# Running sums' rows by DMA through memory, and state space groups outside the job queue

## The chip, the core and the metric

The kernel runs on one core of a Trainium2 chip. The metric is device time in microseconds (us), as the median of several runs. The engines are named PE (TensorE, matmuls), DVE (VectorE), ACT (ScalarE), POOL (GpSimd) and SP (SyncE, which issues most of the DMAs).

## What is computed

Two models are run one after the other on 256 tokens of width 1024, two layers each. The change is in the first. One layer of it projects the normed input and runs three branches, whose gated outputs are projected, summed and added to the residual:

```python
# state space branch, 16 heads in 4 groups, chunks of 128
a_cum = cumsum(dt * a)                          # over the chunk
seg = a_cum[..., :, None] - a_cum[..., None, :]
decay = where(causal, exp(where(causal, seg, 0)), 0)
cb = einsum('bclgn,bcsgn->bgcls', C, B)         # per group
y_diag = einsum(cb * decay, x_dt)               # per head
...
cum = cumsum(log_sigmoid(f_logit + f_bias))
sc = q @ k * scale + cum[query] - cum[key]
probs = softmax(where(causal, sc, -inf)); out = probs @ v
# the third branch is sliding window attention with sinks, without running sums
```

Both running sums are needed twice per element of a 128 x 384 tile (the causal blocks of a 256 x 256 matrix): one as a column, one number per partition, and one as a row that is the same in all partitions. The change is about the rows.

## The kernel before

**Products.** Activations lie with features on partitions. Every product with a weight is taken in split precision: SP loads a unit of weights (8 blocks of 128 by 256 columns, 1 MB) into `wr` (line 123, three buffers), ACT copies it rounded into `wh`, four chunks of 128x512 (line 98), and DVE, for one chunk POOL, subtracts to get `wl` (line 101). `mm3` then makes three matmuls per block, so a unit is 48 matmuls of 128x256. The loads are issued two units ahead of their use.

**Order.** PE keeps the order in which the program is written. What is not a weight product is woven in by ticks: after each 12 matmuls `tick` advances time by 0.5, steps the tasks whose `yield` has run out, and advances the job queue. So one unit of `yield` is 24 matmuls. The other engines' orders come from a scheduler; each engine runs its own order strictly.

**Jobs.** An attention job (`attn4`) for two heads has stages A (scores into PSUM, masked reduction on DVE, exponentials on ACT, normalisation on DVE), B (transposes on PE), 2.5 after A, and C (product with v), 1 after B. Next to B the following job's A is called.

**Running sums.** `steps_task` makes step sizes and log decays (`u`, `y`, 64 x 256), waits with `yield 7`, transposes them on PE, and makes the sums with triangular matmuls. The result `rows` (128 x 384) is kept as two rounded parts, high and low, on separate partitions. A row is spread over all partitions by a matmul with a column of `selr`, a 0/1 matrix: lines 725 to 729 for attention, where the scores are then accumulated on top of it, and line 844 in `group_task`, where `ps` then goes through DVE (line 848, minus the column, at most 0).

**State space groups.** For each of four groups the loop at the end of `b1_layer` computes `xs`, then B and C (`bcm`), then the gate `z`, each a weight unit. `conv` turns the first two into 128x512 tiles: per half one ACT step and three DVE steps, then a tanh on ACT and a last DVE product. Then `group_task` is spawned. It transposes `xs` (line 95), multiplies C with B (`ps<-f`), and hands two jobs to the job queue, which make the decays of two heads each, and in their C stage the product with `xs`, `po<-f,f`. After these come the norm of the group (`rs_r`) and its spreading over partitions (`pt<-cst,rs_r`), which the products with `ya` need.

In the names of the rows, `f` is any tile of the pool `f2` (13 buffers of 128x512 here), `pd`, `ps`, `pt` and `po` are PSUM tiles, `h` is the normed input, `yb` the sliding window branch's output.

Of the kernel before, what the change touches and what calls it, by code (L numbers as in the profile page):

```python
# [24 lines left out]
def _pack(table, items):  # L25
    o = 0
    for name, n in items:
        table[name] = (o, n)
        o += n
    return o  # L30
# [8 lines left out]
NCST = _pack(CST, [("ident", 128), ("tri", 128), ("ntri", 128), ("sel", 32), ("hl", 1),  # L39
                   ("sgn", 1), ("ca", 1), ("cf", 1), ("msel", 24)])  # L40
# [6 lines left out]
class Kern:  # L47
    def __init__(self, ctx, tc, A, out, dbg=None):
        self.tc, self.nc, self.A, self.out = tc, tc.nc, A, out
        self.dbg = dbg or {}  # L50
        nc = tc.nc
        self.V, self.S, self.P, self.T = nc.vector, nc.scalar, nc.gpsimd, nc.tensor
        p = lambda name, bufs, **kw: ctx.enter_context(tc.tile_pool(name=name, bufs=bufs, **kw))
        self.cst_p = p("cst", 1)
        self.w_p = p("w", 3)
        self.wl_p = p("wlo", 3)
        self.x_p = p("x", 1)
        self.m_p = p("wm", 2)
        self.r_p = p("r", 3)
        self.sm_p = p("sm", 2)  # L60
        self.ps_d = p("psd", 3, space=PSUM)
        self.ps_s = p("pss", 2, space=PSUM)
        self.ps_t = p("pst", 2, space=PSUM)
        self.ps_o = p("pso", 1, space=PSUM)
        self.t = self.rows = 0
        self.on_pool = (1024,)
        self.tasks = []
        self.jobs = []
        self.waiting = []
        self.cur = self.nxt = None  # L70
# [123 lines left out]
    def advance(self):  # L194

        c = self.cur
        if c is None:
            if self.jobs:
                self.start()
        elif c.stage == 0:  # L200
            if self.t - c.t >= 2.5:
                if c.B is None:
                    c.C()
                    self.cur = None
                    self.start()
                else:
                    c.B()
                    c.stage, c.t = 1, self.t
                    if self.jobs:
                        self.nxt = self.jobs.pop(0)  # L210
                        self.nxt.A()
                        self.nxt.t = self.t
        elif self.t - c.t >= 1:
            c.C()
            self.cur, self.nxt = self.nxt, None
            if self.cur is None:
                self.start()

    def start(self):
        if self.jobs:  # L220
            self.cur = self.jobs.pop(0)
            self.cur.A()
            self.cur.t = self.t

    def qk(self, pss, cuts, q, k, first):

        for a, b, c, d in cuts:
            for i, ps in enumerate(pss):
                p = slice(64 * i, 64 * i + 64)
                self.mm(ps[:, a:b], q[p, 128 * (a > 0):128 * (a > 0) + 128], k[p, c:d], first, first or b == 384)  # L230
# [68 lines left out]
    def consts(self):  # L299
        nc, A = self.nc, self.A  # L300
        c = self.cst_p.tile([128, NCST], F32, name="cst")
        nc.sync.dma_start(c, A["cst"])
        g = lambda n: c[:, CST[n][0]:CST[n][0] + CST[n][1]]
        self.ident, self.tri, self.ntri = g("ident"), g("tri"), g("ntri")
        self.hl, self.sgn, self.ca, self.cf = g("hl"), g("sgn"), g("ca"), g("cf")
        self.msel = g("msel")
        self.sel = self.cst_p.tile([128, 32], F32R, name="selr")
        self.V.tensor_copy(self.sel, g("sel"))
# [168 lines left out]
class Job:  # L477


    def __init__(self, A, B, C):  # L480
        self.A, self.B, self.C, self.stage, self.t = A, B, C, 0, 0
# [20 lines left out]
def b1_layer(K, l, x, yr, sums, cw, wdt=None, first_sums=None):  # L502
# [41 lines left out]
    rows = K.sm1_p.tile([128, 384], F32R, name="rows")  # L544
# [3 lines left out]
    def steps_task():  # L548
# [5 lines left out]
        if first_sums is not None:  # L554
            yield 4
# [23 lines left out]
        yield 7  # L579
# [17 lines left out]
        rh = K.f2((128, 384), F32R)  # L597
        K.act(rh, ps)
        K.stt(rows, rh.bitcast(F32), K.hl, ps, ALU.mult, ALU.add)
# [19 lines left out]
    def pv2(o, pair, v, pts):  # L619
        for i in range(2):  # L620
            K.mm(o[64 * i:64 * i + 64, pair, :], v(i, 0), pts[i][:, 0:256], True, False)
        for i in range(2):
            K.mm(o[64 * i:64 * i + 64, pair, 128:256], v(i, 1), pts[i][:, 256:384], False, True)

    def attn4(score, v, masks, mn_fix, done, wait=0, until=()):
# [5 lines left out]
        def job(pair):  # L631
            def A():
                mn = K.small([128, 2, 2], "mn")
# [5 lines left out]
                for i, ps in enumerate(pss):  # L639
                    pr = K.f2((128, 384))  # L640
                    for a, s in enumerate((slice(0, 128), slice(128, 384))):
                        K.masked(pr[:, s], ps[:, s], masks[a], mn[:, i, a:a + 1],
                                 3e38 if mn_fix is None else ns[:, i:i + 1])
                    prs.append(pr)
# [17 lines left out]
            def B():  # L662
                pts = []
                for i, pr in enumerate(sh["p"]):
# [8 lines left out]
                    pts.append(pT)  # L673
# [10 lines left out]
            return Job(A, B, C)  # L684
# [13 lines left out]
    for i in range(4):  # L698
# [26 lines left out]
        def score(pair, pss, q=q, kk=kk, i=i):  # L725
            for e, ps in enumerate(pss):
                o = 16 + 4 * i + 2 * pair + e
                K.mm(ps, K.sel[:, o:o + 1].to_broadcast([128, 128]), rows, True, False)
            K.qk(pss, ((0, 128, 0, 128), (128, 384, 0, 256)), q[:, pair, :], kk[:, pair, :], False)

        jc += attn4(score, lambda j, t, v=v: v[:, t, 64 * j:64 * j + 64], (K.msk("u"), K.msk("zero", 2)), None, gated(yc, zs, 2 * i),
                    until=(steps,))

# [48 lines left out]
    for i in range(4):  # L782
# [7 lines left out]
        def score(pair, pss, q=q, i=i):  # L790
            K.qk(pss, ((0, 128, 0, 128), (128, 384, 0, 256)), q[:, pair, :], kk[:, i // 2, :], True)
# [27 lines left out]
    def group_task(g, xs, bcm, zs):  # L819
# [16 lines left out]
        sh = {}  # L836

        def job(pair):
            def A():
                sh["m", pair] = ms = []  # L840
                for i in range(2):
                    hd = 4 * g + 2 * pair + i
                    ps = K.psx((128, 384))
                    K.mm(ps, K.sel[:, hd:hd + 1].to_broadcast([128, 128]), rows, True, True)
                    m = K.f2((128, 384))

                    for t, s in enumerate((slice(0, 256), slice(256, 384))):
                        V.tensor_scalar(m[:, s], ps[:, s], ncum[:, t, hd:hd + 1], 0.0, op0=ALU.add, op1=ALU.min)  # L848
                    K.act(m, m, AF.Exp)
                    K.tt(m, m, cb, ALU.mult)  # L850
                    ms.append(m)

            def C():
                if pair == 0:
                    return
                o = K.po((128, 2, 256))
                for pr in range(2):
                    pv2(o, pr, lambda i, t: xd[:, t, 64 * (2 * pr + i):64 * (2 * pr + i) + 64], sh["m", pr])
                t1 = K.f2((128, 2, 256))
                for c in range(2):  # L860
                    K.stt(t1[:, c, :], xs[:, c, :], vec("dsk", 8 * l + 2 * g + c), o[:, c, :], ALU.mult, ALU.add)
                y = K.k_p.tile([128, 2, 256], F32, name="yg%d" % g, tag="k%d" % g)
                K.stt(y, t1, 0.5, zs, ALU.mult, ALU.mult)
                sh["y"] = y
                K.act(t1, y, AF.Square)
                K.tt(t1[:, 0, :], t1[:, 0, :], t1[:, 1, :], ALU.add, K.P)
                sh["sq"] = t1

            return Job(A, None, C)

        yield 1
        K.enqueue([job(0), job(1)])
        while "sq" not in sh:
            yield 1
        yield 2
        ps = K.pt((128, 2))
        for t in range(2):
            K.mm(ps[:, t:t + 1], sh["sq"][:, 0, t * 128:t * 128 + 128], K.ones[:, 0:1], True, True)
# [4 lines left out]
        K.tt(t1, sh["y"], K.bc(R, 2), ALU.mult)  # L883
# [7 lines left out]
    for g in range(4):  # L891
        xs = conv(K.dense(K.unit(), H, (0, 1)), (2 * g, 2 * g + 1))
        bcm = conv(K.dense(K.unit(), H, (0, 1)), (8 + g, 12 + g))
        zs = gate_z(K.dense(K.unit(), H, (0, 1)))
        gts.append(K.spawn(group_task(g, xs, bcm, zs)))
# [821 lines left out]
def layout(inputs):  # L1717
# [21 lines left out]
    sel = np.zeros((128, 32), f32)  # L1739
    for h in range(16):  # L1740
        sel[[h, 32 + h], h] = 1
        sel[[64 + h, 96 + h], 16 + h] = 1
    p = np.arange(128)
    hl = np.where((p // 32) % 2 == 1, -1, 0).astype(f32)
# [3 lines left out]
    cst = {"ident": I, "tri": (i <= j).astype(f32), "ntri": -(i > j).astype(f32), "sel": sel,  # L1748
           "hl": hl[:, None], "sgn": sgn[:, None], "ca": ca[:, None], "cf": cf[:, None], "msel": (p[:, None] % 32 == np.arange(24)[None, :]).astype(f32)}
# [167 lines left out]
```

## Time and profile before

| what | value |
|---|---|
| median of three runs | 2091.35 us (2088.39 to 2092.54) |
| the profiled execution, and its span | 2090.28 us, 2088.5 us |
| granted clock of PE, mean | 0.995 |
| busy: PE, DVE, ACT, POOL | 2044.8, 1457.0, 991.1, 482.1 us |
| DMA | 326.12 MB, 156 GB/s |
| layer 0, layer 1 state space groups | about 285 to 425 us, 770 to 905 us |

Busy time tells how much an engine did, over stages that have different limits. To know what a change of one stage is worth, the windows of that stage are read, and in it who waits for whom. A timeline row gives the start, the time taken by a group of like instructions (from the first start to the last end), and in brackets how long the engine had been idle before it and what ended that. Matmuls overlap each other by their filling, so distances between starts tell what one costs.

### The profile page before, as it was taken

The page shows a single profiled execution, that of the slowest core. Times are in us where ns is not written, and L with a number is a line of the kernel's source. Part 1 is how long each engine was busy: PE and PEld are TensorE (multiplying, and loading weights), DVE is VectorE, ACT ScalarE, POOL GpSimd, SP SyncE. Part 2 cuts the span into 40 slices and gives each one's busy share as a digit, 9 for nine tenths or more (in the row PEclk, how much of TensorE's full clock was granted, in tenths as well). Part 3 has the DMA queues.
Part 4 walks back from the last instruction along what each step waited for, and adds up shares of the span by engine and source line. Part 5 has one row for each costly group of instructions (what it writes and reads, how often), then busy time and mean ns, then how long its engine had stood idle before and what let it go on. Part 6 is the DMA issues. An engine that isn't in the chain of part 4 may idle for free.

```text
span 2088.5 us, 37547 instructions
## 1 busy us (share of the span) xinstructions
PE 2044.8 (98%) x14832; PEld 1850.8 (89%) x14832; DVE 1457.0 (70%) x2837; ACT 991.1 (47%) x2117; POOL 482.1 (23%) x361
## 2 busy tenths in 40 slices
PE   7999999999999999999999999999999989999998
PEld 7988999998988999999877888888888889999998
DVE  7667788866766778978466454864565566779974
ACT  6455555544454555555244333542333354556553
POOL 3222222323113223233100212111111131232222
PEclk9999999999999999999999999999999999999999
DMA  7645656565646656544111232222322233454552
GB/s 276 247 162 195 229 190 235 182 242 187 232 172 207 218 184 226 192 177 179 59 56 56 86 121 101 89 93 101 101 101 79 83 132 112 144 190 162 184 181 81
DMA packets 52831, 326.12 MB, mean 156 GB/s; under 512 B 6832, under 2 KB 8624, under 8 KB 16304
## 3 DMA queue, kind: packets, MB, share of 16 engines
q1 hardware_dynamic: 48528, 319.26, 43.2%
q10 hardware_dynamic: 4128, 4.46, 0.8%
q8 instruction: 117, 1.92, 0.4%
q14 instruction: 58, 0.48, 0.1%
HBM read 318.72 MB, written 1.05 MB: 153 GB/s over the span
## 4 chain that ended last, share of the span: by engine, by line
PE 89%; DVE 6%; DMA 2%; issue 1%; ACT 1%; ACTq 0%; POOL 0%; SPq 0%; DVEq 0%; POOLq 0%
PE pd L92 77%; PE ps L92 4%; PE po L92 3%; DVE wl L101 2%; PE pt L92 2%; PE pt L95 2%; DMA f<-f 1%; DVE f L101 1%; DVE f L104 1%; ACT wh L98 1%; ACT f L98 0%; DMA wr<-in_w_dram 0%; DVE rq_t L104 0%; DVE f L969 0%; ACTq L1037 0%
## 5 line engine op out<-in xcount | busy, mean ns | idle before, releaser
L101 DVE TENSOR_TENSOR wl<-wr,wh 128x512 fp32r<-128x512 f32 x751 | 676.3, 920 | 253.0 <-ACT wh L98 251.5
L98 ACT ACTIVATE wh<-wr 128x512 fp32r<-128x512 f32 x992 | 561.3, 621 | 531.3 <-PE pd L92 299.0
L101 POOL TENSOR_TENSOR wl<-wr,wh 128x512 fp32r<-128x512 f32 x241 | 351.0, 1456 | 1311.5 <-ACT wh L98 1125.9
L92 PE MATMUL pd<-h,wh 128*128 128x256 f32 x2688 | 497.3, 286 | 1.8 <-ACT wh L98 1.8
L92 PEld LDWEIGHTS pd<-h,wh 128*128 128x128 f32 x2688 | 419.2, 192 | 22.2 <-issue 17.3
L92 PE MATMUL pd<-h,wl 128*128 128x256 f32 x1344 | 380.6, 283 | 2.5 <-DVE wl L101 2.5
L92 PE MATMUL pd<-hh,wh 128*128 128x512 f32 (+1 forms) x992 | 345.9, 349 | 0.1
L92 PE MATMUL pd<-hh,wl 128*128 128x512 f32 (+1 forms) x992 | 339.7, 342 | 3.0 <-DVE wl L101 3.0
L92 PE MATMUL pd<-hl,wh 128*128 128x512 f32 (+1 forms) x992 | 340.0, 343 | 1.9 <-DVE hl L101 1.9
L92 PEld LDWEIGHTS pd<-h,wl 128*128 128x128 f32 x1344 | 258.1, 192 | 2.7 <-DVE wl L101 2.7
L92 PEld LDWEIGHTS pd<-hh,wh 128*128 128x128 f32 x992 | 188.9, 190 | 28.7 <-issue 7.5
L92 PEld LDWEIGHTS pd<-hh,wl 128*128 128x128 f32 x992 | 189.0, 191 | 24.8 <-DVE wl L101 3.4
L92 PEld LDWEIGHTS pd<-hl,wh 128*128 128x128 f32 x992 | 189.1, 191 | 22.8 <-DVE hl L101 2.3
L92 PE MATMUL pd<-act,wh 128*128 128x256 f32 (+1 forms) x688 | 161.9, 329 | 2.7 <-DVE f L104 2.7
L104 DVE SCALAR_TENSOR_TENSOR f<-pd,cw,f 128x255 f32<-128x255 f32 (+3 forms) x272 | 151.2, 556 | 15.7 <-ACT f L98 13.0
L92 PEld LDWEIGHTS pd<-act,wh 128*128 128x128 f32 x688 | 117.4, 192 | 14.0 <-ACT wh L98 2.9
L92 PE MATMUL pd<-mg,wh 128*128 128x256 f32 (+1 forms) x576 | 113.7, 296 | 2.8 <-DVE mg L104 2.1
L92 PE MATMUL pd<-hf,wh 128*128 128x256 f32 x640 | 115.4, 283 | 0.0
L92 PE MATMUL pd<-act,wl 128*128 128x256 f32 (+1 forms) x344 | 112.8, 328 | 0.0
L98 ACT ACTIVATE f<-f,mn 128x128 f32<-128x128 f32 (+2 forms) x160 | 79.7, 500 | 59.6 <-DVE mn L234 59.5
L92 PEld LDWEIGHTS pd<-hf,wh 128*128 128x128 f32 x640 | 99.8, 192 | 0.1
L98 ACT ACTIVATE f<-f 128x512 f32<-128x512 f32 (+4 forms) x92 | 52.3, 568 | 99.5 <-DVE f L848 50.5
(259 smaller groups left out, 3238.7 us busy)
## 6 DMA issues: line engine op xcount, KB each, us to landing
wr<-in_w_dram SPq DMA_DIRECT2D x233, 1024.0 KB, 4.8
wm<-in_wm_dram SPq DMA_DIRECT2D x48, 1024.0 KB, 7.9
wr<-in_wd_dram SPq DMA_DIRECT2D x8, 768.0 KB, 4.2
wr<-in_wa_dram SPq DMA_DIRECT2D x8, 512.0 KB, 3.5
c<-in_c_dram SPq DMA_DIRECT2D x2, 1920.0 KB, 9.3
f<-f ACTq DMA_DIRECT2D x32, 64.0 KB, 2.1
wr<-in_wp_dram SPq DMA_DIRECT2D x8, 256.0 KB, 2.6
wr<-in_wf_dram SPq DMA_DIRECT2D x8, 256.0 KB, 2.6
```

What stands on the lines that cost most here:

```text
L92: self.T.matmul(out, l, r, start=start, stop=stop)
L95: self.T.transpose(out, in_, self.ident[0:k, 0:k])
L98: self.S.activation(out, in_, f, **kw)
L101: (eng or self.V).tensor_tensor(out, a, b, op=op)
L104: self.V.scalar_tensor_tensor(out, a, s, b, op0=op0, op1=op1)
```

## The change

`rows` becomes a plain float32 tile. SP writes it to a tile `far` in device memory, and each row that is wanted is read back by SP with a source that repeats over 128 partitions. `selr` and the high and low parts go.

Attention: a new stage P of a job issues the two copies of its heads (128x384, 196 KB each) and lets POOL add the causal mask to the diagonal blocks. P is called 0.5 after the A of the job ahead, and A not before 2 after P. The scores start their own PSUM group, and the masked reduction takes the copy as its second operand.

State space: the groups no longer use the job queue. `group_task` is spawned before the gate's unit, with a wait of 0.5, and first issues three copies: two of 2 heads by 256 and one of 4 heads by 128. One unit later come the transposes and the product of C and B, then three steps of 0.5 that turn the three copies into decays, each one exponential and one product over 512 columns, and after 1.5 more the product with `xs`. `z` is handed over through a dictionary. In `steps_task` the waits go from 4 to 3 (first layer alone) and from 7 to 5.5.

```diff
     def advance(self):
...
         elif c.stage == 0:
+            if self.t - c.t >= 0.5:
+                self.prepared()
             if self.t - c.t >= 2.5:
-                if c.B is None:
...
-                else:
-                    c.B()
-                    c.stage, c.t = 1, self.t
-                    if self.jobs:
-                        self.nxt = self.jobs.pop(0)
...
+                c.B()
+                c.stage, c.t = 1, self.t
+                if self.prepared():
+                    self.nxt = self.jobs.pop(0)
...
+    def prepared(self):
+        if not self.jobs:
+            return False
+        j = self.jobs[0]
+        if j.P is None:
+            return True
+        if j.since is None:
+            j.P()
+            j.since = self.t
+        return self.t - j.since >= 2
...
-    rows = K.sm1_p.tile([128, 384], F32R, name="rows")
+    rows = K.sm1_p.tile([128, 384], F32, name="rows")
+    far = K.dram_p.tile([128, 384], F32, name="far%d" % l)
+    def spread_row(n):
+        t = K.f2((128, 384))
+        nc.sync.dma_start(t, far[n:n + 1, :].to_broadcast([128, 384]))
+        return t
...
         if first_sums is not None:
-            yield 4
+            yield 3
...
-        yield 7
+        yield 5.5
...
-        rh = K.f2((128, 384), F32R)
-        K.act(rh, ps)
-        K.stt(rows, rh.bitcast(F32), K.hl, ps, ALU.mult, ALU.add)
+        K.act(rows, ps)
+        nc.sync.dma_start(far, rows)
...
+            def P():
+                sh["b"] = [spread_row(row0 + 2 * pair + i) for i in range(2)]
+                for t in sh["b"]:
+                    diag = t.rearrange("p (a b) -> p a b", a=3)[:, 0:3:2, :]
+                    K.tt(diag, diag, K.bc(K.msk("u"), 2), ALU.add, K.P)
...
         def score(pair, pss, q=q, kk=kk, i=i):
-            for e, ps in enumerate(pss):
-                o = 16 + 4 * i + 2 * pair + e
-                K.mm(ps, K.sel[:, o:o + 1].to_broadcast([128, 128]), rows, True, False)
-            K.qk(pss, ((0, 128, 0, 128), (128, 384, 0, 256)), q[:, pair, :], kk[:, pair, :], False)
+            K.qk(pss, ((0, 128, 0, 128), (128, 384, 0, 256)), q[:, pair, :], kk[:, pair, :])
...
-    def group_task(g, xs, bcm, zs):
+    def group_task(g, xs, bcm, zd):
+        dec = []
+        for hs, cs in ((2, slice(0, 256)), (2, slice(0, 256)), (4, slice(256, 384))):
+            h0 = 4 * g + (2 if len(dec) == 1 else 0)
+            t = K.f2((128, hs, cs.stop - cs.start))
+            nc.sync.dma_start(t, far[h0:h0 + hs, cs].unsqueeze(0).to_broadcast([128, hs, cs.stop - cs.start]))
+            dec.append(t)
         yield 1
...
         yield 1
-        K.enqueue([job(0), job(1)])
-        while "sq" not in sh:
-            yield 1
+        for n in (0, 2, 1):
+            m = dec[n]
+            for i in range(m.shape[1]):
+                hd = 4 * g + i + (2 if n == 1 else 0)
+                V.tensor_scalar(m[:, i, :], m[:, i, :], ncum[:, n // 2, hd:hd + 1], 0.0, op0=ALU.add, op1=ALU.min)
+            K.act(m, m, AF.Exp)
+            K.tt(m, m, K.bc(cb[:, 256:384] if n == 2 else cb[:, 0:256], m.shape[1]), ALU.mult)
+            yield 0.5
+        yield 1.5
+        while "z" not in zd:
+            yield 0.5
+        o = K.po((128, 2, 256))
...
         bcm = conv(K.dense(K.unit(), H, (0, 1)), (8 + g, 12 + g))
-        zs = gate_z(K.dense(K.unit(), H, (0, 1)))
-        gts.append(K.spawn(group_task(g, xs, bcm, zs)))
+        zd = {}
+        gts.append(K.spawn(group_task(g, xs, bcm, zd), 0.5))
+        zd["z"] = gate_z(K.dense(K.unit(), H, (0, 1)))
         gate_proj(1, yb, g, jb, False)
```

PE, before, second group of layer 0, at the end of the gate's unit (products with `h`) and the start of the branch projection (products with `yb`). `f_3803` is `xs`, `f_3902` is `bcm`:

```order
L92 MATMUL pd<-h,wh 128x256 x2
L92 MATMUL pd<-h,wl 128x256
L95 MATMUL pt<-cst,f_3803 128x128 x4
L92 MATMUL ps<-f_3902 128x256
L92 MATMUL ps<-f_3902 128x128
L92 MATMUL pd<-yb,wh 128x256 x2
```

PE, after, the same group, 36 matmuls into the unit of z, the first behind the unit of B and C. `f_3847` is `xs`, `f_3930` is `bcm`:

```order
L92 MATMUL pd<-h,wh 128x256 x2
L92 MATMUL pd<-h,wl 128x256
L95 MATMUL pt<-cst,f_3847 128x128 x4
L92 MATMUL ps<-f_3930 128x256
L92 MATMUL ps<-f_3930 128x128
L92 MATMUL pd<-h,wh 128x256 x2
```

The transposes and the product of C and B moved from the end of the gate's unit to 60 matmuls earlier, into z's.

DVE, before, the same group: the convolution of B and C, `f_3893`, to its last product `f_3902`; `po` and `yg` belong to the group ahead:

```order
L101 TENSOR_TENSOR wl<-wr,wh 128x512 x2
L104 SCALAR_TENSOR_TENSOR f_3886<-f_3385,vec_108,po 128x256 x2
L104 SCALAR_TENSOR_TENSOR f_3893<-pd,cw_195,f_3893 128x255
L104 SCALAR_TENSOR_TENSOR yg_3889<-f_3886,f_3561 128x512
L104 SCALAR_TENSOR_TENSOR f_3893<-pd,cw_195,f_3893 128x254
L101 TENSOR_TENSOR wl<-wr,wh 128x512
L104 SCALAR_TENSOR_TENSOR f_3893<-pd,cw_195,f_3893 128x253
L104 SCALAR_TENSOR_TENSOR f_3893<-pd,cw_195,f_3893 128x255
L104 SCALAR_TENSOR_TENSOR f_3893<-pd,cw_195,f_3893 128x254
L104 SCALAR_TENSOR_TENSOR f_3893<-pd,cw_195,f_3893 128x253
L101 TENSOR_TENSOR wl<-wr,wh 128x512 x2
L104 SCALAR_TENSOR_TENSOR f_3902<-f_3902,f_3893 128x512
```

DVE, after, the same convolution, `f_3921`, to its last product `f_3930`:

```order
L101 TENSOR_TENSOR wl<-wr,wh 128x512
L104 SCALAR_TENSOR_TENSOR f_3921<-pd,cw_195,f_3921 128x255
L101 TENSOR_TENSOR wl<-wr,wh 128x512
L104 SCALAR_TENSOR_TENSOR f_3921<-pd,cw_195,f_3921 128x254
L101 TENSOR_TENSOR wl<-wr,wh 128x512
L104 SCALAR_TENSOR_TENSOR f_3921<-pd,cw_195,f_3921 128x253
L104 SCALAR_TENSOR_TENSOR f_3921<-pd,cw_195,f_3921 128x255
L104 SCALAR_TENSOR_TENSOR f_3921<-pd,cw_195,f_3921 128x254
L104 SCALAR_TENSOR_TENSOR f_3921<-pd,cw_195,f_3921 128x253
L101 TENSOR_TENSOR f_3961<-yg_3739,pt 128x512
L104 SCALAR_TENSOR_TENSOR f_3930<-f_3930,f_3921 128x512
```

Skip term and gate of the group ahead have left the place; three chunks of weights' low parts stand between the first steps, and the norm of the group ahead, `f_3961`, before the last product.

PE, before, a second pair of heads of the forgetting attention, layer 0: transposes of the pair ahead, the rows by `selr`, the scores:

```order
L95 MATMUL pt<-cst,f_1245 128x128 x3
L95 MATMUL pt<-cst,f_1248 128x128 x3
L92 MATMUL ps<-rows,selr 128x384 x2
L92 MATMUL ps<-f_552,f_551 128x128 x2
L92 MATMUL ps<-f_552,f_551 128x256 x2
L92 MATMUL pd<-h,wh 128x256 x2
```

PE, after, the same pair; `f_1157` and `f_1159` are the spread rows, which the pair ahead's scores were reduced into:

```order
L95 MATMUL pt<-cst,f_1157 128x128 x3
L95 MATMUL pt<-cst,f_1159 128x128 x3
L92 MATMUL ps<-f_553,f_552 128x128 x2
L92 MATMUL ps<-f_553,f_552 128x256 x2
L92 MATMUL pd<-h,wh 128x256 x2
```

The two matmuls with `selr` are gone, and the order around them stays.

## Rows read from the trace of the kernel before

**Rows 1.** The page: span; then busy us, share of the span, instructions.

```profile
span 2088.5 us, 37547 instructions
...
PE 2044.8 (98%) x14832; PEld 1850.8 (89%) x14832; DVE 1457.0 (70%) x2837; ACT 991.1 (47%) x2117; POOL 482.1 (23%) x361
```

**Rows 2.** Windows: us, PE, PEld, DVE, ACT, POOL busy (x instructions), clock, DMA, GB/s.

```profile
285.00:425.00 140.00, 140.00 (x1165) 131.09 (x1164) 120.67 (x237) 74.65 (x147) 42.67 (x31) 1.00 0.58 211
...
770.00:905.00 135.00, 135.00 (x1122) 126.73 (x1121) 121.61 (x235) 72.11 (x141) 41.31 (x31) 1.00 0.57 205
```

**Rows 3.** Timeline, PE: start us, us, engine line op, out<-in, [idle <-releaser].

```profile
438.23 0.40 PE L92 MATMUL pd<-h,wh 128*128 128x256 f32 x2
438.47 0.28 PE L92 MATMUL pd<-h,wl 128*128 128x256 f32 x1
439.24 0.71 PE L92 MATMUL pt<-cst,rs_r 128*128 128x128 f32 x4 [0.49 <-DVE rs_r L104]
```

**Rows 4.** Instructions of tile selr: duration ns min/median/max, first and last start.

```profile
L92 PE MATMUL ps<-rows,selr x64: 332/338/445, 79.9 to 899.4; 128*128 128x384 f32 x64
```

**Rows 5.** Timeline, PE, a state space pair of the selr matmuls.

```profile
337.21 0.51 PE L92 MATMUL ps<-rows,selr 128*128 128x384 f32 x2
337.56 0.40 PE L92 MATMUL pd<-yb,wh 128*128 128x256 f32 x2
```

**Rows 6.** Timeline, PE, an attention pair of the selr matmuls.

```profile
121.27 0.60 PE L92 MATMUL ps<-rows,selr 128*128 128x384 f32 x2
121.80 0.71 PE L92 MATMUL ps<-f,f 64*128 64x128 f32 x6
```

**Rows 7.** Timeline, PE, transposes of xs and product of C and B.

```profile
333.25 0.60 PE L95 MATMUL pt<-cst,f 128*128 128x128 f32 x4
333.69 0.82 PE L92 MATMUL ps<-f 128*128 128x256 f32 x4
```

**Rows 8.** Timelines, ACT, DVE, POOL, convolution behind an xs unit, layer 1.

```profile
760.08 0.63 ACT L98 ACTIVATE wh<-wr 128x512 fp32r<-128x512 f32 x1 [1.53 <-PE pd L92]
760.62 0.55 ACT L98 ACTIVATE f<-pd,cw 128x256 f32<-128x256 f32 x1
...
766.80 0.63 ACT L98 ACTIVATE f<-f 128x512 f32<-128x512 f32 x1 [1.65 <-DVE f L104]
...
762.76 1.41 DVE L101 TENSOR_TENSOR wl<-wr,wh 128x512 fp32r<-128x512 f32 x1
...
765.19 1.52 DVE L104 SCALAR_TENSOR_TENSOR f<-pd,cw,f 128x255 f32<-128x255 f32 x3 [0.63 <-ACT f L98]
...
767.47 0.69 DVE L104 SCALAR_TENSOR_TENSOR f<-f,f 128x512 f32<-128x512 f32 x1 [0.29 <-ACT f L98]
...
762.34 1.28 POOL L101 TENSOR_TENSOR wl<-wr,wh 128x512 fp32r<-128x512 f32 x1 [6.62 <-ACT wh L98]
```

**Rows 9.** Timelines, ACT and DVE, the same in layer 0, first, last.

```profile
312.07 0.63 ACT L98 ACTIVATE wh<-wr 128x512 fp32r<-128x512 f32 x1 [0.20 <-PE pd L92]
...
319.88 0.69 DVE L104 SCALAR_TENSOR_TENSOR f<-f,f 128x512 f32<-128x512 f32 x1 [0.76 <-ACT f L98]
```

**Rows 10.** Timelines, DVE and PE, layer 1's step sizes and their transposes.

```profile
538.81 1.27 DVE L578 TENSOR_SCALAR f<-f,ac 64x256 f32<-64x256 f32 x1
...
542.46 0.46 PE L95 MATMUL pt<-cst,f 64*128 64x64 f32 x4
```

**Rows 11.** The page: DMA issues, number, KB each, us to landing.

```profile
wr<-in_wd_dram SPq DMA_DIRECT2D x8, 768.0 KB, 4.2
...
wr<-in_wp_dram SPq DMA_DIRECT2D x8, 256.0 KB, 2.6
```

**Rows 12.** Timelines, DVE and PE, an attention pair, normalisation and transposes.

```profile
580.44 0.35 DVE L660 TENSOR_SCALAR f<-f,den 128x256 f32<-128x256 f32 x1
...
582.56 0.71 PE L95 MATMUL pt<-cst,f 128*128 128x128 f32 x5
```

**Rows 13.** Waits of SP's queue: us in total, times, longest us.

```profile
SPq L123 <- DVE wl L101: 1826.4, 259, 27.2
```

## What is predicted for the change

> **What bounds the kernel now.** I read the page first: TensorE (PE) is busy 2044.8 of the 2088.5 us that the span lasts [rows 1]. Such a share can hide stages with another limit, so I then took the windows of the two stretches with the state space groups, one for each layer: 140.00 of 140.00 us and 135.00 of 135.00 us of PE [rows 2]. PE stands still nowhere there. VectorE (DVE) is at 86% and 90%, which no average of the whole shows, and ScalarE (ACT) at 53%. Two things follow for this change. A matmul taken out of these stretches shortens the kernel by what it holds PE. A wait put onto PE there lengthens it by its whole length, since nothing in the stretch waits today that could absorb it. PE keeps the order in which the program is written, so what stands behind a waiting matmul waits too.
>
> The unit of time below is the dense matmul of 128x256: two of them start 0.24 us before the next one, so 0.12 us each [rows 3], and a weight unit of 48 takes 5.76 us.
>
> **Matmuls that go.** The broadcast of the running sums was 64 matmuls with `selr`, two for each pair of heads: 16 pairs of the forgetting attention, 16 of the state space groups, over both layers [rows 4]. By duration they are 338 ns each, but matmuls overlap, so I take starts: in a state space pair the next matmul starts 0.35 us after the pair did (337.21 to 337.56) [rows 5]. In an attention pair it is 0.53 us (121.27 to 121.80) [rows 6], but there the transposes ahead of it would have to drain in any case. I take 0.35 for all 32 pairs: -11.2 us. The upper bound takes 0.53 for the 16 attention pairs: -14.1 us.
>
> **The wait that it brings: C times B.** In the kernel before, a group's four transposes of `xs` and its product of C and B stand behind the whole gate unit; now they stand 36 matmuls into the z unit, the first unit after that of B and C. The product needs `bcm`, and `bcm` comes out of a convolution on ACT and DVE that can only begin when the B and C unit is through. So this is a race, and both runners have rows.
>
> PE: the 36 matmuls take 4.32 us. The four transposes take 0.44 us (333.25 to 333.69) [rows 7], and two more of the same shape, which spread the previous group's norm, about 0.22. That is 5.0 us from the first matmul of the z unit, which starts about 0.2 us before ACT is released by the end of the unit ahead: PE is there 4.8 us after the release.
>
> The convolution: the trace has the same thing behind an `xs` unit, with the same order of work as the changed kernel has for `bcm`: one weight chunk on ACT, which waits for PE, then the first convolution step, three weight chunks with their low parts on DVE between the steps, three steps in a row, the tanh, the last product. It starts at 760.08 and its last product ends at 767.47 + 0.69 = 768.16: 8.08 us after the release [rows 8]. A second one goes from 312.07 to 320.57, 8.5 us, with an exponential in between [rows 9]. So PE waits 8.08 - 4.8 = 3.3 us, or 3.7 by the second one.
>
> What could shorten it: the third low part took 1.41 us beside a weight chunk on GpSimd (POOL) of 1.28 us [rows 8], while a DVE operation of the same size with two operands took 0.69 undisturbed [rows 8]; without that overlap the chain is 0.7 shorter and the wait 2.6. And with no weight work between the steps at all it is one chunk and the chain by itself: 0.54 + 0.55 + 1.52 + 0.55 + 1.52 + 0.63 + 0.69 = 6.0, with gaps about 6.2 us, a wait of 1.4. I take 3.0 us, nearest to the measured form, with 1.4 and 3.7 as ends. There are eight groups: +24 us, from 11 to 30.
>
> The Trainium skill, page "SBUF — State Buffer", section "SBUF: two separate sides", has a rule for that overlap: a DVE operation with two SBUF operands and a GpSimd operation that reads SBUF take the shared port pair by an exclusive lock for the whole instruction, so the later one is blocked entirely. By that rule each group pays as often as POOL's chunk starts first; with it always so the sum would be about 2 us higher than mine, with it never so about 3 us lower. The row of 1.41 us beside 1.28 us agrees with it.
>
> **What else moves.** Layer 1's step sizes are needed earlier: the wait of seven became five and a half, which is 36 matmuls, 4.32 us. Their last operation ended at 538.81 + 1.27 = 540.08, and the transposes of them stood at 542.46 [rows 10], now at 538.14: a wait of 1.9 us. In layer 0 the operands have spare time by the same reckoning, so nothing.
>
> At the end of each layer's groups PE waited for the last group's norm, 0.49 us before `pt<-cst,rs_r` at 439.24 [rows 3], and again in layer 1, with a similar length. The last group's norm now comes over one weight unit sooner, so both go: -1.0 us. Next in line there is the branch's own product, whose weights wait in their buffers.
>
> The rows for the attention (16 copies of 196 KB in each layer) must have landed, and have the mask added by POOL, before the scores' reduction. 256 KB land 2.6 us after issue [rows 11]; the copies are issued two units of time ahead, but four of them are queued on SyncE (SP) behind a weight load or freed buffer and have about 24 matmuls and a product. The tightest pair of today ends its last normalisation at 580.44 + 0.35 and has 1.8 us in hand until 582.56, where the transposes start [rows 12]. So I take +0.5 us over all, with 0 and 5.6 (0.35 in each of 16 pairs, all that the matmuls there took) as ends. The state space groups' three copies are 768 KB a group, 4.2 us by the weight load of that size [rows 11], and their use comes 120 matmuls later: hidden, with a rival below. Weight loads queue behind all these on SP; but SP itself waits for free weight buffers 1826.4 us in 259 waits [rows 13], so a load is held back by full buffers and not by its queue, and a delay of a few us is covered. Were that cover gone, each delayed unit would cost up to a copy's 2.6 us. The mask additions, 32 on POOL, fall on an engine with much idle time and cost nothing except by the overlap above. DVE reads copies in SBUF in place of PSUM: off the path.
>
> **Sum**, against the profiled execution's own 2090.28 us, of which 1.8 lie outside its span: 2090.28 - 11.2 - 1.0 + 24 + 1.9 + 0.5 = 2104.5. That execution is 1.07 us below the median of the three runs shown (2091.35); with that put back, 2105.5, and I say **2105 us**. With the wait at C times B at 2.4 to 3.7 us it is 2100 to 2111.
>
> **Rivals.**
> *The convolution runs at its bare length.* DVE's low parts give way and the wait is the 1.4 us above: 11 us in place of 24, so 2091.3 + 1.07, about 2092: the removed matmuls and the new waits cancel. For it: DVE loses work in this stretch (reads of PSUM, one exponential's row fewer). Against it: the order still has three low parts between the steps.
>
> *The wait is short enough that the gain remains* (the other side). Break-even is where eight waits and 2.4 us equal 12.2 us: 1.2 us each. Below 0.7 us each the kernel is faster by over 0.2%; with 0.5 us each it is 2084.5 on the profiled time, 2085.5 at the median. This would take a `bcm` ready 5.3 us after the release, less than the bare chain of 6.2, so PE would have to be late itself: held ahead of the transposes by something that I don't see, which then is no loss added but shifted. Or the pairs' 14.1 us of the upper bound and the bare chain together, 2089. Little in the trace speaks for it.
>
> *The decays come late.* The three copies stand behind two weight loads on SP. If they leave one weight unit late (5.76), land 4.2 later [rows 11] and then pass eight subtractions of about 0.35 [rows 12], the exponentials of about 0.63 and products of about 0.69 [rows 8], some 6 us, they are ready after 16 us. The use is 120 matmuls, 14.4 us, plus the wait at C times B, 3 us, behind their tick: 1.4 us in hand. Another 3.4 us of delay makes each group wait 2 us: 2121. For it: SP's queue is in order. Against: SP runs ahead.
>
> *The broadcast doesn't get cheaper*: the attention's copies are late and PE stands at the scores' transposes in place of the matmuls: the 5.6 us of the upper end, 2110.
>
> **How the numbers follow.** My forecast has 0.58, the bare chain 0.20, the faster case 0.12, late decays 0.06, late attention rows 0.04. A measurement of this kernel can tell about 0.2%, 4.2 us, from no change. The forecast's whole band, late decays and late rows are slower: 0.68. The bare chain is within the bound: 0.20. The rest is faster: 0.12. The range goes from 2086, which leaves out most of the faster case (0.1), to 2114, which leaves out the later decays and the top of the waits (0.08).
>
> **What would show it.** In the profile of the changed kernel PE should wait for DVE `f` at `ps<-f` eight times, about 3 us each, where the stretches had no idle time; the `selr` rows are gone; the wait for `rs_r` before the products with `ya` is gone in both layers; and one wait for the step sizes' transposes stands in layer 1. The forecast is wrong if the eight waits are below 1.5 us, if they stand at `po<-f,f` (late decays) or at `pt<-cst,f` (late rows), or if PE's busy time falls by much more than 11 us.

## The result, and the profile after

The changed kernel takes 2114.24 us (median of 4 runs, 2111.3 to 2122.17) against 2089.97 us of the kernel before on the same occasion; the ratio is 1.0116, with a 95% interval of 1.0097 to 1.0134. The direction was right, and the time lies 0.24 us above the range's upper end of 2114 and 9 us above the forecast of 2105: the change cost 24 us where 14 were forecast.

The profiled execution of the changed kernel is the slowest of its four, 2122.17 us, so its rows carry a little more than the median does. From its page, the lines that answer to [rows 1], with the chain of work that ended last:

```profile
span 2120.4 us, 37598 instructions
PE 2050.9 (97%) x14768; PEld 1857.1 (88%) x14768; DVE 1465.7 (69%) x2826; ACT 991.3 (47%) x2109; POOL 503.1 (24%) x393
...
PE 81%; DVE 13%; ACT 2%; issue 2%; DMA 1%; ACTq 0%; POOL 0%; SPq 0%; DVEq 0%; POOLq 0%
```

PE's busy time rose by 6 us although 64 matmuls went, and the share of DVE in the chain went from 6% to 13%. The waits of PE say where (engine, line, what it waited for: us in total, times, longest):

```profile
PE ps L92 <- DVE f L104: 27.3, 8, 4.0
...
PE pt L92 <- DVE rs_r L104: 5.2, 4, 2.4
...
PE po L92 <- DVE f L692: 1.9, 1, 1.9
...
PE pt L95 <- DVE f L682: 1.3, 1, 1.3
...
PE pt L95 <- DVE f L593: 0.6, 1, 0.6
```

The first row is the wait at C times B: eight times, 27.3 us, where [rows 2] had stretches without any. One of them in layer 0, as timelines of ACT, DVE, POOL and PE, in this order:

```profile
327.35 0.63 ACT L98 ACTIVATE wh<-wr 128x512 fp32r<-128x512 f32 x1 [0.24 <-PE pd L92]
...
334.08 0.63 ACT L98 ACTIVATE f<-f 128x512 f32<-128x512 f32 x1 [1.65 <-DVE f L104]
...
330.02 1.42 DVE L101 TENSOR_TENSOR wl<-wr,wh 128x512 fp32r<-128x512 f32 x1
...
332.47 1.52 DVE L104 SCALAR_TENSOR_TENSOR f<-pd,cw,f 128x255 f32<-128x255 f32 x3 [0.63 <-ACT f L98]
...
334.74 0.69 DVE L104 SCALAR_TENSOR_TENSOR f<-f,f 128x512 f32<-128x512 f32 x1 [0.16 <-ACT f L98]
...
329.60 1.30 POOL L101 TENSOR_TENSOR wl<-wr,wh 128x512 fp32r<-128x512 f32 x1 [6.32 <-ACT wh L98]
...
331.97 0.60 PE L95 MATMUL pt<-cst,f 128*128 128x128 f32 x4
335.49 1.22 PE L92 MATMUL ps<-f 128*128 128x256 f32 x2 [2.92 <-DVE f L104]
```

ACT is released at 327.35 and the last product ends at 334.74 + 0.69 = 335.43, 8.08 us later, to the hundredth the length of the chain in [rows 8]; the low part beside POOL's chunk is there too, 1.42 us. PE begins its transposes at 331.97; with the 0.44 us that they take [rows 7] it is at C times B 5.1 us after the release, where I had 4.8, and waits 2.92 us.

In layer 1 three of the four waits are 4.00 us. There the tanh of the `xs` convolution stands on ACT between the weight chunk, which is released at 818.88, and the first step for B and C, which comes at 820.41 in place of some 0.54 us after the release, so the whole chain is 1 us late:

```profile
818.88 0.63 ACT L98 ACTIVATE wh<-wr 128x512 fp32r<-128x512 f32 x1 [0.65 <-PE pd L92]
819.88 0.63 ACT L98 ACTIVATE f<-f 128x512 f32<-128x512 f32 x1 [0.37 <-DVE f L104]
820.41 0.55 ACT L98 ACTIVATE f<-pd,cw 128x256 f32<-128x256 f32 x1
...
828.02 1.22 PE L92 MATMUL ps<-f 128*128 128x256 f32 x2 [4.00 <-DVE f L104]
```

The other thing that no term of the sum had is in the windows around the first wait of layer 1 (us; PE, PEld, DVE, ACT, POOL busy; granted clock; DMA):

```profile
776.00:782.00 6.00, 5.99 (x48) 4.97 (x45) 5.50 (x9) 4.04 (x8) 1.30 (x1) 1.00 0.25 104
782.00:786.00 4.00, 0.85 (x8) 0.61 (x6) 2.54 (x6) 1.19 (x2) 0.00 (x0) 0.99 0.61 186
786.00:793.00 7.00, 6.45 (x29) 6.26 (x30) 4.23 (x9) 2.86 (x6) 0.97 (x2) 0.52 0.52 157
793.00:823.00 30.00, 30.00 (x255) 27.83 (x254) 23.70 (x49) 14.09 (x27) 9.33 (x7) 1.00 0.57 211
```

PE stands for 3.70 us until 786.55, and right after that the granted clock is 0.52, which is the 1.2 GHz level for nearly all of the 7 us; PE does about half the work that it did before. In matmuls (PE's timeline):

```profile
787.85 0.77 PE L92 MATMUL pd<-h,wh 128*128 128x256 f32 x2
788.43 0.41 PE L92 MATMUL pd<-h,wl 128*128 128x256 f32 x1
788.64 0.63 PE L92 MATMUL pd<-h,wh 128*128 128x256 f32 x2
789.07 0.41 PE L92 MATMUL pd<-h,wl 128*128 128x256 f32 x1
```

From 788.43 to 789.07 are three matmuls, 0.21 us each in place of 0.12 [rows 3]. Such a fall lasted 6.8 us behind each wait of layer 1, and in layer 0 6.8 and 3.4 us behind the first and the second; behind the other two there was none. The kernel before has no fall in these stretches (clock 1.00 in both rows of [rows 2]). By these prices a fall of 6.8 us holds some 32 matmuls where 57 would have stood, an estimate of 3 us lost. Five of these and a short one are 16 us, of which a little lay in the waits themselves. The falls are not the same in every execution: in the profile of a kernel with the same order of work (the first try at the chain, below) the same eight waits have five falls behind them, three of 3.4 us and two of 6.8 us.

The Trainium skill, page "TensorE: Matmul & The Clock Gate", section "HAM oscillation — how this bites in real kernels", says that waits of PE for data can send its clock to the half rate, so that the next stretch of work starts cold, each time anew. These windows agree, with 0.52 behind the wait and 1.00 ahead of it, though not each time: two of the eight waits have no fall behind them.

### The profile page after: what moved, and what is told of

The parts are those of the page before. It is cut to its first block, busy times and chain, and to the rows that moved or that the text cites. A ratio compares the mean times of both kernels' runs of the same rounds, so it can differ in the third digit from the quotient of the medians.

```text
span 2120.4 us, 37598 instructions
## 1 busy us (share of the span) xinstructions
PE 2050.9 (97%) x14768; PEld 1857.1 (88%) x14768; DVE 1465.7 (69%) x2826; ACT 991.3 (47%) x2109; POOL 503.1 (24%) x393
## 4 chain that ended last, share of the span: by engine, by line
PE 81%; DVE 13%; ACT 2%; issue 2%; DMA 1%; ACTq 0%; POOL 0%; SPq 0%; DVEq 0%; POOLq 0%
PE pd L92 71%; DVE wl L101 5%; DVE f L104 4%; PE ps L92 4%; PE po L92 3%; PE pt L92 2%; PE pt L95 2%; ACT f L98 1%; DVE f L101 1%; ACT wh L98 1%; DVE f L980 0%; DMA wr<-in_w_dram 0%; DVE h L104 0%; DVE hl L101 0%; DVE act L101 0%
## 5 line engine op out<-in xcount | busy, mean ns | idle before, releaser
L101 POOL TENSOR_TENSOR wl<-wr,wh 128x512 fp32r<-128x512 f32 x241 | 344.8, 1431 | 1242.1 <-ACT wh L98 1115.7
L92 PE MATMUL pd<-h,wh 128*128 128x256 f32 x2688 | 508.4, 290 | 1.9 <-ACT wh L98 1.8
L92 PEld LDWEIGHTS pd<-h,wh 128*128 128x128 f32 x2688 | 428.4, 196 | 24.6 <-issue 19.9
L92 PE MATMUL pd<-h,wl 128*128 128x256 f32 x1344 | 385.2, 287 | 2.5 <-DVE wl L101 2.5
L92 PEld LDWEIGHTS pd<-h,wl 128*128 128x128 f32 x1344 | 263.1, 196 | 2.7 <-DVE wl L101 2.7
L98 ACT ACTIVATE f<-pd,cw 128x256 f32<-128x256 f32 (+1 forms) x120 | 66.9, 557 | 67.0 <-DVE f L104 60.5
```

The lines of the kernel that those rows point to most:

```text
L92: self.T.matmul(out, l, r, start=start, stop=stop)
L98: self.S.activation(out, in_, f, **kw)
L101: (eng or self.V).tensor_tensor(out, a, b, op=op)
```

## The experiments

**The changed kernel with the waits filled.** If the falls of the clock come from PE standing idle, and cost time of their own, then PE must be held equally long but work. Ahead of each product of C and B:

```diff
         ps = K.psx((128, 384))
+        for _ in range(28):
+            K.mm(ps[:, 0:256], H[0](0)[:, 0:128], H[0](0), True, True)
         K.mm(ps[:, 0:256], bcm[:, 0, 0:128], bcm[:, 1, :], True, True)
```

> The changed kernel with 28 more matmuls of 128x256 (3.4 us) ahead of each product of C and B, written into its PSUM tile and overwritten by it: PE is held as long as before but works instead of waiting. Theory that the idle waits also lower the granted clock and that this costs time of its own: the clock returns to 0.993 or more and the time falls to 2102 to 2108 us although PE has 27 us more of work. Rival, the clock's falls are by chance or cost nothing: the time stays at 2111 to 2116 us.

Measured: 2108.71 us (4 runs), ratio 1.0071 (1.0054 to 1.0088). The upper end of the theory's band was passed by 0.7 us; the clocks are 0.991 to 0.994, a little under what was expected. In the same session a kernel with the order of work of the changed one (below) took 2118.5 us.

**The same three ways on one chip**: the changed kernel, the filled one, and one with 14 matmuls in each wait.

> The changed kernel once more, beside the next two on the same chip, for the size of what the granted clock takes. Theory, the eight waits are followed by falls of the clock: 2112 to 2120 us, clock 0.984 to 0.990, and the time of its executions goes with their clock. Rival, the earlier difference between it and the kernel with filled waits was one of chips or chance: no more than 3 us between this and the next.

> The kernel with 28 matmuls in each of the eight waits once more. Theory: 6 to 11 us below the run of the changed kernel beside it, with a clock of 0.991 to 0.995, though PE is held as long at the same eight places. Rival: within 3 us of it.

> The same with 14 matmuls (1.7 us) in each of the eight waits, so that PE still stands idle for 1.2 us in layer 0 and 2.3 us in layer 1. Theory that the clock falls with the longer idle times: falls in layer 1 only or fewer of them, a time between the two others, 2108 to 2113 us. Rival, any wait of PE there lowers the clock as much: the time of the changed kernel.

Measured: 2115.4 us (ratio 1.0108, 1.0091 to 1.0125), 2105.18 us (1.0064, 1.0047 to 1.0082) and 2116.56 us (1.0118, 1.0099 to 1.0137), beside 2093.61 us of the kernel before. So the filled kernel is 10.2 us faster than the changed one though it gives PE 27 us of useless work, and the intervals are apart. By the ratios it is 9.2 us, give or take some 5. It is rather too little than too much, since the filled kernel holds PE about 2 us longer at these places: 28 matmuls take 3.4 us where most waits of layer 0 were 2.9 us, and in layer 1 four waits of up to 0.7 us are left. The windows of layer 1's groups, of the changed, the filled and the half filled kernel:

```profile
770.00:935.00 165.00, 149.23 (x1152) 137.63 (x1152) 127.59 (x252) 75.30 (x144) 41.43 (x32) 0.92 0.56 193
```

```profile
770.00:925.00 155.00, 152.60 (x1264) 141.64 (x1264) 126.08 (x252) 75.26 (x144) 41.68 (x32) 1.00 0.59 206
```

```profile
770.00:925.00 155.00, 145.89 (x1184) 134.93 (x1183) 125.33 (x241) 73.51 (x141) 42.42 (x32) 0.98 0.56 194
```

The granted clock there is 0.92, 1.00 and 0.98. The half filled kernel missed its expectation: its profiled execution shows only two falls of 3.4 us in the groups, behind waits of 2.35 us in layer 1 and none behind 1.26 us in layer 0, but its median is no better than that of the unfilled one. Its other executions have clocks of 0.988 to 0.990, like the changed kernel's (0.985 to 0.989) and unlike the filled one's (0.991 to 0.996). How a wait's length decides on a fall is therefore not settled; that filling the eight waits gives back about 10 us is, in two pairs of runs.

**The early place alone, in the kernel before.** Only the spawning of the task was moved; rows by `selr` and the job queue stay:

```diff
-        zs = gate_z(K.dense(K.unit(), H, (0, 1)))
-        gts.append(K.spawn(group_task(g, xs, bcm, zs)))
+        zd = {}
+        gts.append(K.spawn(group_task(g, xs, bcm, zd), 0.5))
+        zd["z"] = gate_z(K.dense(K.unit(), H, (0, 1)))
```

> The kernel before with one part of the change alone: the group's task is spawned before the gate's unit with a wait of 0.5, so the transposes and the product of C and B stand 36 matmuls into the z unit; rows by selr and the job queue stay. Theory: the place alone makes the waits, 2.5 to 4 us in each of eight groups, and lowers the clock: 2113 to 2130 us. Rival, the waits need the copies or the new order of decays: 2088 to 2093 us.

Measured: 2124.2 us, ratio 1.015 (1.0135 to 1.0166), with this row of PE's waits:

```profile
PE ps L92 <- DVE f L104: 27.9, 8, 4.0
```

Eight waits, 27.9 us, without any copy: the place alone makes them. It costs 32 us, against 27.9 us of waits; in its profile the clock falls behind five of the eight.

**The place moved back, in two steps.** The first yield of `group_task` was 1. With 2.5 (and the last wait before the product with `xs` 0.5 in place of 1.5):

> The changed kernel with the transposes of xs and the product of C and B 36 matmuls later (first yield of group_task 2.5 in place of 1; the last wait before the product with xs is 0.5 in place of 1.5, so that this comes 12 matmuls later only). Theory: the eight waits of PE at ps<-f (27.3 us in the profile of the changed kernel) vanish, and with them the falls of the granted clock in those stretches: 2077 to 2086 us, clock 0.993 or more. Rival, the copies and the decays out of the job queue cost the time and the wait only moves: the waits show up at po<-f,f, 2095 us or more.

Measured: 2090.3 us (10 runs), ratio 0.9994 (0.9981 to 1.0007). Neither theory had it whole: three waits at C times B are left in layer 1, and seven at `po`, six of them at `po<-f,f` in the groups of layer 0, small where the rival had them large. The rows of one, DVE's and PE's timeline, and the waits:

```profile
807.18 1.52 DVE L104 SCALAR_TENSOR_TENSOR f<-pd,cw,f 128x255 f32<-128x255 f32 x3 [0.63 <-ACT f L98]
808.62 2.36 DVE L101 TENSOR_TENSOR wl<-wr,wh 128x512 fp32r<-128x512 f32 x2
810.89 0.68 DVE L104 SCALAR_TENSOR_TENSOR f<-f,f 128x512 f32<-128x512 f32 x1
...
811.63 0.92 PE L92 MATMUL ps<-f 128*128 128x256 f32 x4 [2.01 <-DVE f L104]
```

```profile
PE ps L92 <- DVE f L104: 6.0, 3, 2.0
...
PE po L92 <- DVE f L101: 3.4, 7, 0.9
```

PE comes 4.3 us later, and now two low parts (2.36 us, one beside POOL) stand ahead of the convolution's last product, so half of what was given is used up in these three groups. That the scheduler puts them there because the product is wanted later is my reading; no run tests it. With 3.5, where the kernel before had the product:

```diff
             dec.append(t)
-        yield 1
+        yield 3.5
```

> The changed kernel with the first yield of group_task 3.5 in place of 1: transposes, the product of C and B and all that follows stand 60 matmuls later, at the end of the gate's unit, where the kernel before had the product. Theory: no wait at ps<-f and none at po<-f,f is left in the groups, the clock is that of the kernel before, and the removed matmuls show: 2079 to 2087 us where the kernel before has 2092. Rival, the copies and the other new waits eat the gain wherever the product stands: 2088 us or more, as in the run with 36 matmuls.

Measured: 2076.92 us (6 runs, 2072.75 to 2080.77), ratio 0.9926 (0.9912 to 0.994): faster than both kernels. The windows, to be held against [rows 2], show PE without a gap again:

```profile
285.00:425.00 140.00, 140.00 (x1176) 130.55 (x1174) 115.10 (x237) 75.21 (x144) 45.42 (x32) 1.00 0.67 237
760.00:905.00 145.00, 145.00 (x1212) 135.13 (x1209) 123.94 (x254) 77.77 (x150) 42.69 (x33) 1.00 0.64 224
```

**The two halves of the change.** The attention's rows by copies, groups as before; and the groups with the product at the late place, attention as before. Both have the new waits of `steps_task`, and in both the copied rows hold the rounded high part of the sums only.

> The kernel before with the attention's rows by copies and the changed waits of steps_task alone; state space groups as before, with selr and the job queue. The copied row holds the rounded high part of the sums only. Theory: 32 matmuls gone, -5.6 us, against new waits of 3 to 4 us that the changed kernel shows at 103, 550 and 644 us: 2088 to 2091 us where the kernel before has 2092. Rival, the copies are on time in all but those places and the matmuls were dearer (0.53 us a pair): 2084 to 2087 us.

> The state space part alone, with its product of C and B 60 matmuls later as in the run beside it; the attention's rows by selr as in the kernel before; the copied rows hold the rounded high part of the sums only. Theory: 32 matmuls gone, -5.6 us, no wait in the groups: 2084 to 2088 us where the kernel before has 2092. Rival, the groups' copies or later norms cost as much: 2090 us or more.

Measured: 2086.91 us, ratio 0.9971 (0.996 to 0.9982), 6.1 us gained; and 2080.8 us, 0.9943 (0.9928 to 0.9957), 11.9 us gained, each more than its theory had. The sum is 18, the two together gave 15.5 (12.6 to 18.4). The first time lies in the band of its rival, by which a pair of attention matmuls costs 0.53 us. The rows say otherwise. From the transposes to the next weight product, in the kernel before and in the one with the attention's part alone:

```profile
111.45 0.82 PE L95 MATMUL pt<-cst,f 128*128 128x128 f32 x6
...
113.41 0.39 PE L92 MATMUL pd<-h,wh 128*128 128x256 f32 x1
```

```profile
112.44 0.82 PE L96 MATMUL pt<-cst,f 128*128 128x128 f32 x6
...
114.04 0.50 PE L93 MATMUL pd<-h,wh 128*128 128x256 f32 x2
```

That is 1.96 us and 1.60 us: a pair was worth 0.36 us here too, and the rest of the 6.1 us is not explained by it.

**The chain shortened, first try.** The convolution of B and C was given priority in the scheduler.

> The changed kernel with the convolution of B and C given priority in the order of ACT and DVE, so that the weights' chunks stand behind its steps. Theory, the weights' low parts between the steps make the chain long: the waits at ps<-f fall from 3.4 to 1.4 to 2.0 us each and the clock falls less, 2092 to 2102 us. Rival, the chain's own length rules: waits stay above 3 us, 2111 us or more.

Measured: 2118.5 us, ratio 1.0117 (1.0094 to 1.014), but neither theory was tested: the order of ACT and DVE came out as it was, the waits too. It served as a repetition of the changed kernel.

**The chain shortened, second try.** The low parts of the weight unit that is split beside the convolution all go to POOL:

```diff
-        zd["z"] = gate_z(K.dense(K.unit(), H, (0, 1)))
+        K.on_pool = (0, 512, 1024, 1536)
+        w = K.unit()
+        K.on_pool = (1024,)
+        zd["z"] = gate_z(K.dense(w, H, (0, 1)))
```

> The changed kernel with the low parts of the weight unit that is split beside the convolution of B and C all on POOL, so that no part of it stands between the convolution's steps on DVE. Theory, the low parts make 1.5 to 2 us of the chain: the eight waits fall from 27 to 12 to 16 us, 1.4 to 2.4 us each, the clock falls less, 2094 to 2103 us. Rival, the chain's own length rules, or late low parts become the wait at pd<-wl: 2108 us or more.

Measured: 2098.96 us (10 runs), ratio 1.0034 (1.0022 to 1.0046). The waits, and the chain of one group (ACT's release, DVE's last product):

```profile
PE ps L92 <- DVE f L104: 15.3, 8, 2.7
```

```profile
323.78 0.63 ACT L98 ACTIVATE wh<-wr 128x512 fp32r<-128x512 f32 x1 [0.24 <-PE pd L92]
...
327.05 1.52 DVE L104 SCALAR_TENSOR_TENSOR f<-pd,cw,f 128x255 f32<-128x255 f32 x3 [0.63 <-ACT f L98]
...
329.32 0.74 DVE L104 SCALAR_TENSOR_TENSOR f<-f,f 128x512 f32<-128x512 f32 x1 [0.16 <-ACT f L98]
```

The chain goes from 323.78 to 330.06, 6.28 us in place of 8.08, and the waits fall to 15.3 us. So the three low parts between its steps made 1.8 us of the chain, and the time followed: by the ratios 15 to 17 us less than the changed kernel and its repetitions, with 12 us less of waiting. PE's waits for low parts at `pd` are 6.2 us, as in the kernel before, so the rival of late low parts fell.

## Why the prediction was right, and where it failed

**The wait at C times B: right in place, number and mechanism, a little small.** Eight waits, forecast at 3.0 us each within 1.4 to 3.7, came to 3.4 on the average: 2.8 to 2.9 in layer 0, 3.7 to 4.0 in layer 1. The chain was the 8.08 us that I had read, overlap with POOL included; the 0.3 us that I took off for an overlap that might be missing was made good by PE being 0.3 us later than I reckoned. Layer 1's extra microsecond is the tanh ahead on ACT; I had one length for all eight groups, from a convolution that had no tanh in that place. Together +3.3 us.

**The step that failed** is in the first paragraph: "A wait put onto PE there lengthens it by its whole length". It lengthened the kernel by more, since the waits lower the granted clock for the matmuls that follow. The sum had no term for it, and neither did the range. The pair of filled and unfilled waits puts it at 10.2 us (9.8 in the session before, against the repetition of the changed kernel). That is about the whole distance from forecast to result, the other departures nearly cancelling. The trace of before had the warning, in windows outside the groups (columns as above):

```profile
500.00:600.00 100.00, 99.28 (x810) 89.89 (x812) 68.33 (x152) 49.92 (x120) 24.21 (x17) 0.98 0.53 189
2000.00:2088.00 88.00, 76.05 (x617) 75.38 (x615) 48.18 (x79) 34.53 (x69) 23.41 (x19) 0.95 0.35 120
```

The clock is 0.98 and 0.95 where PE's busy time leaves 0.7 and 12 us open. I had read the 1.00 of the groups, and of the stretches with waits only such as had short ones, under 1 us.

**The removed matmuls: right.** 0.35 us for a pair is what the late kernel shows in the groups, and 0.36 us is what the attention rows above show, so the upper bound of 0.53 us was not needed: in layer 0 the products with `yb` begin at 300.64, 335.07, 369.51 and 403.93 us, 34.4 us apart, in the kernel before at 299.58, 334.26, 369.37 and 404.49, which in the last two distances is 35.1: 0.7 us less for two pairs. The gain of the whole without the eight waits is larger than the 9.8 us of my other terms, though: 15.5 us (12.6 to 18.4). The `rs_r` waits at the ends of the groups are gone as forecast [rows 3]. Part of the difference is a wait between the groups of the two layers that I didn't look at, in the kernel before and in the changed one:

```profile
500.37 0.45 PE L92 MATMUL po<-yr,f 128*64 128x256 f32 x2 [1.26 <-ACT f L98]
```

```profile
512.32 0.45 PE L92 MATMUL po<-yr,f 128*64 128x256 f32 x2 [0.17 <-ACT f L98]
```

In the kernel before the clock is 0.64 from 501.2 to 505 us, behind this wait; in the changed kernel it stays at 1.00, and so it does in the late kernel. With the attention's part alone the wait is still there, so it is the groups' part that takes it away: by these numbers an estimate of 2.5 us, 1.1 of wait and 1.4 of clock. I have not traced the rest. So the departures work against each other: forecast, waits, attention and step sizes (below) and the clock's 10 us make some 29 us, where 24 were measured.

**Step sizes in layer 1: right in kind, too dear.** The wait is 0.6 us (row `PE pt L95 <- DVE f L593`) where I had 1.9. With the attention's part alone it is 1.9 us; why the whole change has less was not traced.

**Attention rows: within the ends, but six times the 0.5 us.** Two waits, 1.9 and 1.3 us, where I had 0.5 in all. The longer one, at `po`, is for a copy of transposed probabilities that stands on DVE behind low parts; from 103 to 106 us, behind it, the granted clock is 0.54, so it too costs more than itself. The shorter one answers a term that I had put at nothing, the mask additions on POOL (POOL's and DVE's timeline of the changed kernel):

```profile
639.41 1.12 POOL L101 TENSOR_TENSOR f<-f,mask 128x256 f32<-128x256 f32 x1
640.50 1.29 POOL L101 TENSOR_TENSOR f<-f,rope 128x512 f32<-128x512 f32 x1
...
641.82 0.69 DVE L101 TENSOR_TENSOR swk<-swk,f 128x512 f32<-128x512 f32 x1 [1.82 <-POOL f L101]
```

A product of the sliding window branch stands on POOL behind them, DVE waits 1.82 us for it, and behind that on DVE stands the normalisation that PE's transposes wait for. In the kernel before, POOL has no such additions and DVE does not wait there. No run moves the additions elsewhere, so this is read from the rows and not tested. The spread rows themselves were slower than I took them to be (page of the changed kernel, DMA issues: number, KB, us to landing):

```profile
f<-far SPq DMA_DIRECT2D x32, 192.0 KB, 4.9
f<-far SPq DMA_DIRECT2D x24, 256.0 KB, 6.0
```

4.9 us, where I took 2.6 from a weight load of 256 KB [rows 11]. The attention alone still gained 6.1 us, and the scores' reduction ahead of the 1.3 us wait did not wait for a row, so the rival of late rows fell, and that of late decays too: no wait at `po<-f,f` in the groups of the changed kernel.

**The rivals.** The bare chain was real as a length, 6.28 us against my 6.2, but not what the changed kernel had. The faster case needs the product at another place; there it is what the late kernel is.

## What to carry to other kernels

Where an engine keeps the written order and has no idle time, moving an instruction earlier is a race against its operands: take both runners' times from rows, with the work that other queues interleave. A new idle time of PE isn't paid once: look at the granted clock behind the waits that the trace already has, and put what that costs into the sum and the range. And where a scheduler orders the other engines, look at its order anew after giving slack: here half of it went to other work. An engine with much idle time is not free either, where its order puts new work ahead of something that others wait for.

## What the hardware showed unexpectedly

Waits of 2.8 to 4.0 us on PE were followed by 3.4 or 6.8 us at half clock in six of eight cases of the profiled execution; with the waits filled by useless matmuls the kernel was 10 us faster. The small copies with a repeated source landed 4.9 us (192 KB) and 6.0 us (256 KB) after issue, longer than the 4.8 us of a whole weight unit of 1 MB; most of them were issued right behind such a load, and how much of it is that was not separated.
